# The adaLN modulation formed in two halves of the channels at the start of a hybrid conv and attention block

## The chip, the core and the metric

The kernel runs on one core of a Trainium2 chip. TensorE (PE) multiplies, VectorE (DVE), ScalarE (ACT) and GpSimd (POOL) do the rest, and SyncE (SP) and ACT issue most DMAs. The metric is the device time of one execution in microseconds; three runs gave 2390.78, 2391.32 and 2394.15, median 2391.32.

## The reference

One decoder block over 2048 tokens of 1024 channels in float32. What matters here is its beginning:

```python
mod = jax.nn.silu(c) @ w_ada + b_ada
shift, scale, gate = jnp.split(mod, 3, axis=-1)
h = (rms_norm(x, norm_w) * (1.0 + scale[:, None]) + shift[:, None]).astype(dt)
z = h @ w_in                     # (2048, 1024) @ (1024, 10240)
q = rope(rms_norm(q, q_norm_w), positions); k = rope(rms_norm(k, k_norm_w), positions)
```

`c` is one row of 1024, `w_ada` is 1024 x 3072; shift and scale, 2048 columns, are needed before any `h`. From `z` come a convolution branch, 12 attention heads of 128 channels in three groups of dilated windows, and the gates; two projections, the gated sum, `w_out` and the residual end the block.

## The kernel before

The contraction over 1024 channels is cut into KC = 8 slices of 128. A product in float32 is made of three with rounded parts: `h` and the weights are split into an upper part (`hi`, `wh`) and the remainder (`lo`, `wl`), and hi.wh + hi.wl + lo.wh are summed, 24 matmuls (name `pz`, line 373) for 128 tokens and the q, k and v of one head, 384 columns.

The order of PE is written out by hand (a manual schedule); the other engines are filled by a scheduler from the program order and from marks such as `keep_in_program_order`. A *unit* is one head, a *step* j is 128 tokens of it: unit 0 has 16 steps, and each step's `pz` is followed by squares on ACT (390), the power -1/2 on POOL (`rsqrt_cols`, 114 and 115), q and k norm and the rotation on DVE (404 to 414) and a store `qkv_d`. Tokens come in pairs of tiles: `load_x` loads x, squares it (261) and scales it by its norm (269) on ACT; `h_turn` transposes 256 tokens of two slices on PE (279) into a bank; `h_part` (and `h_first` for the first 256 tokens) modulates it out of the bank into `hf` on DVE (302; 290), rounds it to `hT_hi` on ACT (305; 285), subtracts for `hT_lo` (306; 292, half of these on POOL) and stores `hf` to `h_d` from SP. `hf` has two buffers. In unit 0 the parts for tokens j + 2 are made between the matmuls of step j.

The start: SP loads c, b_ada and norm_w as rows (`nat`), 16 blocks of w_ada (128 x 1024 each; two per slice), the positions and the frequencies; ACT's queue loads x0 to x3 and three blocks of w_in (`raw`). silu(c) is a column `sc` per slice. Of the eight slices of w_ada five are multiplied on PE, 1 x 512 into each of four banks (`ada`, 201); three are summed on DVE (192, 194) and then multiplied by a column of ones. Four copies on ACT (221) bring the row into SBUF, sixteen transposes (224) turn it into columns and two DVE operations give `mod` (225, 226). DVE also makes the angles of the rotary tables (`tab`, 165 to 175), ACT their sines (212, 213). Then the whole of `h` for the first 256 tokens is formed, in four calls of `h_first`, and step 0 begins. At its end unit 0 loads and splits the weights of unit 1 (343, 349, 352) through three `raw` buffers.

Of the kernel before, what the change touches and what calls it, by code (L numbers as in the profile page):

```python
# [10 lines left out]
F32 = mybir.dt.float32  # L11
# [43 lines left out]
def tile_hybrid_block(  # L55
# [67 lines left out]
    with pool("start", side="right") as st:  # L123
        keep = tc.keep_in_program_order
        nat = st.tile([4 * KC, P], F32, name="nat")
        cols = st.tile([P, 4 * KC], F32, name="cols")
        keep(nc.sync.dma_start(nat[:KC, :], c.rearrange("b (k p) -> (b k) p", p=P)))
        keep(nc.sync.dma_start(nat[KC : 3 * KC, :], b_ada[: 2 * D].rearrange("(k p) -> k p", p=P)))
        keep(nc.sync.dma_start(nat[3 * KC :, :], norm_w.rearrange("(k p) -> k p", p=P)))
        pos_i = st.tile([P, NB], I32, name="pos_i")  # L130
        freq = st.tile([P, 64], F32, name="freq")
        was = {}

        def ada_load(k):
            for half in range(2):
                wa = was[k, half] = st.tile([P, D], F32, tag="wa", name=f"wada{k}_{half}", bufs=10)
                last = keep(nc.sync.dma_start(wa, w_ada[P * k : P * k + P, D * half : D * half + D]))
            return last

        ada_load(0)  # L140
        keep(nc.sync.dma_start(pos_i, positions.rearrange("b (j p) -> p (b j)", p=P)))
        keep(nc.sync.dma_start(freq, inv_freq[None, :].to_broadcast([P, 64])))
        for k in range(1, KC):
            last_ada = ada_load(k)

        pt = bank("t", "pt_c")
        nc.tensor.transpose(pt[:, : 4 * KC], nat, ident[: 4 * KC, : 4 * KC])
        keep(nc.vector.tensor_copy(cols, pt[:, : 4 * KC]))
        th = consts.tile([P, KC], F32, name="th_c")
        with tc.high_priority():  # L150
            nc.scalar.activation(th, cols[:, :KC], AF.Tanh, scale=0.5)
        keep(nc.vector.scalar_tensor_tensor(sc, th, 1.0, cols[:, :KC], op0=ALU.add, op1=ALU.mult))
        keep(nc.vector.tensor_scalar(sc, sc, 0.5, None, op0=ALU.mult))

        pos_f = st.tile([P, NB], F32, name="pos_f")
        keep(nc.vector.tensor_copy(pos_f, pos_i))
        a = tab[:, :, 0, :]
        n = tab[:, :, 1, :]
        na = st.tile([P, NB, 64], F32, name="na")

        def angles():

            v = nc.vector

            yield v.tensor_tensor(a, pos_f[:, :, None].to_broadcast([P, NB, 64]),
                                  freq[:, None, :].to_broadcast([P, NB, 64]), op=ALU.mult)
            yield v.tensor_scalar(n, a, 1.0 / (2 * math.pi), MAGIC, op0=ALU.mult, op1=ALU.add)
            yield v.tensor_scalar(n, n, -MAGIC, None, op0=ALU.add)
            yield v.tensor_scalar(na, n, MAGIC * 2048, None, op0=ALU.add)
            yield v.tensor_scalar(na, na, -MAGIC * 2048, None, op0=ALU.add)  # L170
            yield v.tensor_sub(n, n, na)
            for part in TWO_PI:
                for t in (na, n):
                    yield v.scalar_tensor_tensor(a, t, -part, a, op0=ALU.mult, op1=ALU.add)
            yield v.tensor_scalar(a, a, -PI_LO, PI_LO, op0=ALU.max, op1=ALU.min)

        turning = angles()

        def angle_steps(count):
            for _, ins in zip(range(count), turning):  # L180
                keep(ins)


        BY_SUM = (1, 3, 5)
        acc = [bank("z", "ada0"), bank("z", "ada1"), bank("s", "ada2"), bank("s", "ada3")]
        sums = st.tile([P, 2 * D], F32, name="sums")

        def ada_sum(k):
            for half in range(2):
                part, wa = sums[:, D * half : D * half + D], was.pop((k, half))  # L190
                if k == BY_SUM[0]:
                    keep(nc.vector.tensor_scalar(part, wa, sc[:, k : k + 1], None, op0=ALU.mult))
                else:
                    keep(nc.vector.scalar_tensor_tensor(part, wa, sc[:, k : k + 1], part, op0=ALU.mult, op1=ALU.add))

        def ada_row(k):
            for half in range(2):
                wa = sums[:, D * half : D * half + D] if k is None else was.pop((k, half))
                col = ones[:, :1] if k is None else sc[:, k : k + 1]
                for i in range(2):  # L200
                    last_row = nc.tensor.matmul(acc[2 * half + i][:1, :], col, wa[:, 512 * i : 512 * i + 512],
                                                start=(k == 0), stop=(k == KC - 1))
# [12 lines left out]
        keep(nc.vector.tensor_scalar(a, a, -2.0, 1.0, op0=ALU.mult, op1=ALU.add))
        last_mm = {k: ada_row(k) for k in (0, 2, 4, None, 6, 7)}
        row = st.tile([1, 2 * D], F32, name="row")

        for i in range(4):
            with tc.issue_after(sin.ins):  # L220
                last_row = nc.scalar.activation(row[:, 512 * i : 512 * i + 512], acc[i][:1, :], AF.Copy)
        pa = bank("z", "pt_ada")
        for k in range(2 * KC):
            nc.tensor.transpose(pa[:, k : k + 1], row[:, P * k : P * k + P], ident[:1, :1])
        keep(nc.vector.tensor_add(mod, pa[:, : 2 * KC], cols[:, KC : 3 * KC]))
        keep(nc.vector.scalar_tensor_tensor(mod[:, KC:], mod[:, KC:], 1.0, cols[:, 3 * KC :], op0=ALU.add, op1=ALU.mult))
    hpool_c = [tc.tile_pool(name=f"hT{i}", bufs=1, side="right", reuse_waits="tile") for i in range(2)]
    hpools = [c.__enter__() for c in hpool_c]

    def quarter_tile(kh, t, hl, name, dtype=F32R):  # L230

        return hpools[0 if t == 0 or (kh, t) == (0, 2) else 1].tile([P, 4, 512], dtype, tag=f"h{hl}{kh}{t}", name=name)

    hi, lo = ({(kh, t): quarter_tile(kh, t, hl, f"hT_{hl}_{kh}{t}") for kh in range(2) for t in range(4)} for hl in ("hi", "lo"))

    def part(x, k, t0, w, nk=1):

        q = x[k // 4, t0 // 512]
        ks = k % 4 if nk == 1 else slice(k % 4, k % 4 + nk)
        return q[:, ks, t0 % 512 : t0 % 512 + w]  # L240
# [8 lines left out]
    def load_x(j, eng=nc.sync):  # L249
# [3 lines left out]
        if j >= 4:  # L253
            tc.keep_in_program_order(i0)
# [1323 lines left out]
```

## Time and profile before

| | us |
|---|---|
| median of three runs | 2391.32 |
| the profiled execution's own time | 2388.53 |
| its span in the profile | 2386.7 |
| PE busy, whole span | 2343.6 |
| first `pz` starts | 45.76 |
| step 4 of unit 0 starts | 73.90 |
| unit 1 starts | 139.55 |
| unit 1's step 1 starts | 147.73 |

All times in rows count from the span's start. A row of a timeline has the start, the duration, the engine, the line of the kernel, the operation, what it writes and reads with its shape, and in square brackets how long the engine was idle before it and what it waited for. Consecutive matmuls overlap, so the distance of their starts is the pace, not the duration. A row of the waits has the total, the number and the longest.

### The profile page before, as it was taken

The page shows a single profiled execution, that of the slowest core. Times are in us where ns is not written, and L with a number is a line of the kernel's source. Part 1 is how long each engine was busy: PE and PEld are TensorE (multiplying, and loading weights), DVE is VectorE, ACT ScalarE, POOL GpSimd, SP SyncE. Part 2 cuts the span into 40 slices and gives each one's busy share as a digit, 9 for nine tenths or more (in the row PEclk, how much of TensorE's full clock was granted, in tenths as well). Part 3 has the DMA queues.
Part 4 walks back from the last instruction along what each step waited for, and adds up shares of the span by engine and source line. Part 5 has one row for each costly group of instructions (what it writes and reads, how often), then busy time and mean ns, then how long its engine had stood idle before and what let it go on. Part 6 is the DMA issues. An engine that isn't in the chain of part 4 may idle for free.

```text
span 2386.7 us, 38725 instructions
## 1 busy us (share of the span) xinstructions
PE 2343.6 (98%) x12353; PEld 2088.3 (87%) x12353; DVE 1737.6 (73%) x4091; ACT 1024.4 (43%) x2850; POOL 843.8 (35%) x1003
## 2 busy tenths in 40 slices
PE   6999999999999999999999999999999999999999
PEld 2989999999999999998888888788888888878887
DVE  5865655555555777777699999979977778887654
ACT  4833433333444554456444444644444444333221
POOL 4421111111111111112577778755556730000221
PEclk9999999999999999999999999999999999999999
DMA  7633544544552222225545445744443569876552
GB/s 260 219 119 109 162 123 143 156 149 155 161 164 81 66 80 59 60 84 163 174 141 165 162 159 194 232 129 152 150 150 124 173 193 333 287 256 205 186 168 102
DMA packets 354106, 378.56 MB, mean 159 GB/s; under 512 B 29737, under 2 KB 251209, under 8 KB 353903
## 3 DMA queue, kind: packets, MB, share of 16 engines
q1 hardware_dynamic: 316414, 316.64, 42.1%
q10 hardware_dynamic: 37488, 59.46, 7.2%
q8 instruction: 98, 1.61, 0.3%
q14 instruction: 106, 0.86, 0.1%
HBM read 235.34 MB, written 140.64 MB: 158 GB/s over the span
## 4 chain that ended last, share of the span: by engine, by line
PE 89%; DVE 3%; DMA 3%; ACT 2%; POOL 1%; issue 1%; SPq 0%; ACTq 0%; DVEq 0%; POOLq 0%
PE pz L373 31%; PE paab L899 7%; PE yc L1207 5%; PE pcab L899 4%; PE pag_mc_d L899 4%; PE oa L1489 4%; PE pag_g_d L899 3%; PE ya L1207 3%; PE pag_ma_d L899 3%; PE po L502 3%; PE ps L453 3%; PE pcg_g_d L899 2%; PE oc L1489 2%; PE pbab L899 2%; PE paag L899 2%; PE pcg_mc_d L899 2%
## 5 line engine op out<-in xcount | busy, mean ns | idle before, releaser
L373 PE MATMUL pz<-wh_u,hT_lo 128*128 128x384 f32 x1536 | 537.6, 350 | 5.3 <-DVE hT_lo L292 3.8
L373 PE MATMUL pz<-wh_u,hT_hi 128*128 128x384 f32 x1536 | 518.9, 338 | 4.2 <-ACT wh_u L349 2.2
L373 PE MATMUL pz<-wl_u,hT_hi 128*128 128x384 f32 x1536 | 519.8, 338 | 0.6 <-DVE wl_u L352 0.4
L114 POOL TENSOR_SCALAR st<-st 128x2 f32<-128x2 f32 x192 | 48.3, 251 | 810.5 <-ACT sq L390 810.5
L404 DVE SCALAR_TENSOR_TENSOR qk<-pz,st,wqk 128x128 f32<-128x128 f32 x384 | 116.9, 346 | 272.3 <-POOL st L115 271.3
L373 PEld LDWEIGHTS pz<-wh_u,hT_lo 128*128 128x128 f32 x1536 | 289.6, 189 | 8.1 <-DVE hT_lo L292 4.6
L373 PEld LDWEIGHTS pz<-wh_u,hT_hi 128*128 128x128 f32 x1536 | 290.6, 189 | 6.6 <-ACT wh_u L349 2.8
L373 PEld LDWEIGHTS pz<-wl_u,hT_hi 128*128 128x128 f32 x1536 | 289.7, 189 | 1.8 <-DVE wl_u L352 1.3
L445 ACT ACTIVATE qkT<-ptq 128x256 f32<-128x256 f32 x192 | 73.9, 385 | 358.3 <-PE ptq L438 305.0
L977 DVE SCALAR_TENSOR_TENSOR ce<-us,pair_taps,ce 128x512 f32<-128x512 f32 x240 | 180.6, 753 | 6.4
L948 DVE SCALAR_TENSOR_TENSOR ce<-ut,chan,ce 128x512 f32<-128x512 f32 x240 | 178.9, 745 | 0.0
L863 POOL TENSOR_TENSOR slT<-wT,shT 128x512 fp32r<-128x512 f32 x107 | 143.9, 1346 | 79.9 <-ACT shT L862 76.7
L961 DVE SCALAR_TENSOR_TENSOR cq<-ut,chan,cq 128x512 f32<-128x512 f32 x208 | 155.3, 747 | 1.0
L862 ACT ACTIVATE shB<-wB 128x512 fp32r<-128x512 f32 x130 | 82.0, 631 | 161.3 <-PE paab L899 51.7
L390 ACT ACTIVATE sq<-pz 128x128 bf16<-128x128 f32 x384 | 105.9, 276 | 90.1 <-PE pz L373 80.8
L115 POOL TENSOR_TENSOR st<-st,mhalf 128x2 f32<-128x2 f32 x192 | 137.6, 717 | 16.0
L862 ACT ACTIVATE shT<-wT 128x512 fp32r<-128x512 f32 x110 | 69.4, 631 | 162.9 <-POOL wT L854 29.0
L863 POOL TENSOR_TENSOR slB<-wB,shB 128x512 fp32r<-128x512 f32 x85 | 111.2, 1309 | 76.9 <-ACT shB L862 76.2
L502 PE MATMUL po<-lv,pT 128*128 128x128 f32 x596 | 96.6, 273 | 0.0
L502 PEld LDWEIGHTS po<-lv,pT 128*128 128x128 f32 x596 | 91.0, 189 | 0.6 <-issue 0.5
L411 DVE TENSOR_TENSOR t<-qk,tab 128x256 f32<-128x256 f32 x192 | 82.4, 429 | 5.5
L863 POOL TENSOR_TENSOR slT<-wB,shT 128x512 fp32r<-128x512 f32 x57 | 74.9, 1321 | 27.7 <-ACT shT L862 27.7
(742 smaller groups left out, 6145.2 us busy)
## 6 DMA issues: line engine op xcount, KB each, us to landing
wB<-in_w_in_dram SPq DMA_DIRECT2D x154, 256.0 KB, 3.4
qkv_d<-qkv SPq DMA_DIRECT2D x128, 192.0 KB, 2.2
wT<-tT_d SPq DMA_DIRECT2D x88, 256.0 KB, 2.6
raw_u<-in_w_in_dram SPq DMA_DIRECT2D x93, 192.0 KB, 3.1
tT_d<-wB ACTq DMA_DIRECT2D x66, 256.0 KB, 2.2
lqk<-qkv_d SPq DMA_DIRECT2D x128, 128.0 KB, 2.2
acc_d<-osb SPq DMA_DIRECT2D x128, 65.0 KB, 1.9
part<-acc_d ACTq DMA_DIRECT2D x64, 130.0 KB, 2.2
```

The lines of the kernel that those rows point to most:

```text
L115: nc.gpsimd.tensor_tensor(dst, scratch[:, :n], mhalf[:, :n], op=ALU.pow)
L373: nc.tensor.matmul(pz[:, :width], part(a, k, P * j, P), w[:, :width], start=(m == 0), stop=(m == 23))
L404: nc.vector.scalar_tensor_tensor(qk[:, 2 * i : 2 * i + 2].rearrange("p a b -> p (a b)"), pz[:, P * i : P * i + P], st[:, 2 + i : 3 + i], w ...
L502: nc.tensor.matmul(po[:, :P], box["pT"][:, P * i : P * i + P], vt, start=(i == 0), stop=(i == nk - 1))
L862: nc.scalar.activation(h, q[name], AF.Copy)
L863: eng.tensor_tensor(l, q[name], h.bitcast(F32), op=ALU.subtract)
L899: nc.tensor.matmul(ps, w, x, start=(m == 0 and ps.name not in first), stop=(m == 11 and not more), skip_group_check=True)
L948: stt(box["e"], e[:, 1 + j : 513 + j], chan[:, cb, 2 * j : 2 * j + 1], box["e"], op0=ALU.mult, op1=ALU.add)
L961: stt(box["o"], o[:, 2 + j : 514 + j], w, psum_o, op0=ALU.mult, op1=ALU.add)
L977: stt(dst, box["both"][:, 1 + j : 513 + j], pair_taps[:, cb, j : j + 1], box["e"], op0=ALU.mult, op1=ALU.subtract if j == 0 else ALU.add)
L1207: nc.tensor.matmul(pz, w, xx, start=(m == 0), stop=(m == len(terms) - 1))
L1489: nc.tensor.matmul(ps, y, w, start=(m == 0 and ps.name not in begun), stop=(m == 11 and not more), skip_group_check=True)
```

## The change

The column vectors of shift and scale are formed by halves of the channels: half g holds channels 512g to 512g + 511 of both. A block of w_ada is now one slice's 512 shift and 512 scale columns of one half (512 KB, two runs of 2 KB a row). The stationary operand is `sc` copied to 32 columns (`wide`), and the 1024 results of a half go as four pieces of 256 columns to partitions 0, 32, 64 and 96 of one bank; one copy on ACT, two transposes on PE and the two DVE operations give that half of `mod`. Nothing is summed on DVE any more. All eight slices of the first half are loaded first; the blocks of w_in for unit 0, x2 to x5 and the second half's slices follow on SP's queue, and x0 and x1 stand at its head.

Between the halves PE transposes and multiplies what the first half's four slices of `h` allow for 512 tokens: steps 0 to 3 have a bank each (`first_pz`), and their matmuls go over two slices and two steps at a time. The rest follows behind the second half. The first half of tokens 4 and 5 is formed there as well. The positions are loaded as 16 rows and turned together with `nat`; the angles are made in two halves of 8 tiles, the second finished inside unit 0's steps. x0 to x5 are scaled half on ACT and half on DVE. The floats of the first 256 tokens have ten tiles of their own (borrowed from the pool `wk`), those of tokens 2 to 5 lie where w_ada landed. Unit 0 uses four banks for `pz`. From token 6 on the store of `hf` is issued by ACT. Of unit 1's blocks of w_in the first three are issued at the start, as before, and four more have tiles of their own.

```diff
+    def ada_load(g, k):
+        keep(nc.sync.dma_start(landed_ada(g, k), w_ada[P * k : P * k + P, : 2 * D].rearrange("p (s c) -> p s c", s=2)
+                               [:, :, 512 * g : 512 * g + 512]))
...
+    first_x(0)
+    first_x(1)
+    for k in range(2):
+        raw_load(k)
+    for k in range(KC):
+        ada_load(0, k)
+    for k in range(2, 4):
+        raw_load(k)
+    first_x(2)
+    first_x(3)
...
+    for k in range(4, KC):
+        raw_load(k)
+    for k in range(5):
+        ada_load(1, k)
+    first_x(4)
+    first_x(5)
+    for k in range(5, KC):
+        ada_load(1, k)
...
+    keep(nc.vector.tensor_copy(wide, sc[:, :, None].to_broadcast([P, KC, 32])))
...
+    def ada_mm(g, acc, k):
+        for q in range(4):
+            nc.tensor.matmul(acc[32 * q : 32 * q + 32, :256], wide[:, k], landed_ada(g, k)[:, q // 2, 256 * (q % 2) : 256 * (q % 2) + 256],
+                             start=(k == 0), stop=(k == KC - 1))
+
+    def ada_mod(g, acc, tag):
+        keep(nc.scalar.activation(rows[g], acc[:, :256], AF.Copy))
+        pa = bank(tag, f"pt_ada{g}")
+        for i in range(2):
+            nc.tensor.transpose(pa[:, P * i : P * i + P], rows[g][:, P * i : P * i + P], ident)
...
-                hf = xp.tile([P, 2, 256], F32, tag="hf", name=f"hf0_{k}", bufs=2)
+            order((nc.sync if order is keep else nc.scalar).dma_start(h_d[2 * kk : 2 * kk + 2, :, P * j : P * j + 256].rearrange("a p t -> p a t"), hf))
...
+    def first_z(j0, kk):
+        for m in range(3):
+            x, w = ((hi, "h"), (hi, "l"), (lo, "h"))[m]
+            for j in (j0, j0 + 1):
+                for k in (2 * kk, 2 * kk + 1):
+                    nc.tensor.matmul(first_pz[j][:, :384], part(x, k, P * j, P), split_w[w, k],
+                                     start=(k == 0 and m == 0), stop=(k == KC - 1 and m == 2))
...
+    ada_mod(0, acc, "o")
+    h_first(0)
+    first_w(2)
+    first_w(3)
+    h_first(1)
+    pair_square(2)
+    pair_square(3)
+    first_pz = [bank("z", f"pz0_{j}") for j in range(2)]
+    for kk in range(2):
+        first_z(0, kk)
+    angle_steps(1, 2)
+    for k in range(4, 6):
+        first_w(k)
+    pair_mean(2)
+    pair_scale(2)
+    pair_scale(3)
...
+    ada_mm(1, acc, 0)
+    h_parts(2, [(kk, h_turn(2, kk)) for kk in range(2)], keep)
+    for k in range(1, 4):
+        ada_mm(1, acc, k)
...
+    for kk in range(2):
+        first_z(2, kk)
...
+    ada_mm(1, acc, 4)
+    h_parts(4, [(kk, h_turn(4, kk)) for kk in range(2)], keep)
+    for k in range(5, KC):
+        ada_mm(1, acc, k)
...
+    ada_mod(1, acc, "o")
+    h_first(2)
+    h_first(3)
+    first_z(0, 2)
...
+            pz = bank("zzss"[j % 4] if u == 0 else "z", f"pz{n}")
...
-                    parts = (0, 1) if j % 2 == 0 else (2, 3)
+                    parts = () if j < 4 else (0, 1) if j % 2 == 0 else (2, 3)
...
+                    more_raw = open_side("rx")
+                if u == 0 and j == NB - 3:
+                    nxt, loads = unit_weights(1)
+                    for m, k in ((6, 0), (12, 1), (18, 2)):
+                        extra.setdefault(m, []).append(lambda k=k: early[-1](k))
```

In all three pairs below a name's last number is only its buffer's. PE from the first to the second half of the modulation: before, one modulation (`pt_ada`), then step 0.

```order
L201 MATMUL ada_174<-wada_1_159,sc 1x512
L224 MATMUL pt_ada<-ident,row 128x1 x16
L373 MATMUL pz_0_450<-wh_u_0_349,hT_hi_256 128x384
L373 MATMUL pz_0_450<-wl_u_0_350,hT_hi_256 128x384
L373 MATMUL pz_0_450<-wh_u_1_355,hT_hi_256 128x384
```

Now, with the rows between left out, `ada_260` being the first half's bank and `ada_392` the second's:

```order
L318 MATMUL ada_260<-first_lo_143,first_hi_134 32x256 x4
L325 MATMUL pt_ada_304<-ident,first_hi_134 128x128 x2
L381 MATMUL pz_0_341<-wh_u_0_241,hT_hi_199 128x384
...
L381 MATMUL pz_1_342<-wh_u_3_321,hT_lo_200 128x384
L318 MATMUL ada_392<-first_hi_136,first_hi_134 32x256 x4
L292 MATMUL pt_x_0_397<-ident,x_167 128x128
...
L381 MATMUL pz_3_444<-wh_u_3_321,hT_lo_200 128x384
L318 MATMUL ada_392<-first_lo_140,first_hi_134 32x256 x4
...
L325 MATMUL pt_ada_530<-ident,first_hi_134 128x128 x2
L381 MATMUL pz_0_341<-wh_u_4_369,hT_hi_201 128x384
```

Half of the matmuls of steps 0 to 3 have moved ahead of the second `pt_ada`, among the second half's slices. From step 4's first matmul on, all 11,145 rows of PE are the same in both.

ACT around step 2's squares, where x7 is scaled (`x_524`; `x_442` is x5 before). Before:

```order
L390 ACTIVATE sq_0_504,st_0_505<-pz_0_450 128x128 x2
L400 ACTIVATE qkv_0_508<-pz_0_450 128x128
L261 ACTIVATE xn_444,xst_445<-x_442 128x512
L305 ACTIVATE hT_hi_256<-hf_0_473 128x2x256
L269 ACTIVATE x_438<-x_438,xst_441 128x512
```

Now:

```order
L577 ACTIVATE sq_2_724,st_2_725<-pz_2_443 128x128
L266 ACTIVATE xn_716,xst_575<-x_573 128x512
L367 ACTIVATE hT_hi_613<-first_lo_140 128x2x256
L274 ACTIVATE x_524<-x_524,xst_526 128x512 x2
L577 ACTIVATE sq_2_724,st_2_725<-pz_2_443 128x128
L274 ACTIVATE x_573<-x_573,xst_575 128x512 x2
L587 ACTIVATE qkv_2_728<-pz_2_443 128x128
L266 ACTIVATE xn_741,xst_578<-x_576 128x512
L577 ACTIVATE sq_3_749,st_3_750<-pz_3_444 128x128
L367 ACTIVATE hT_hi_473<-hf_0_783 128x2x256
L371 DMA h_d<-hf_0_783 128x2x256
```

The scale of x7 stands behind step 2's first square and the last `hT_hi` of tokens 4 (`hT_hi_613`), and each `hT_hi` from token 6 on is followed by the store of its `hf`.

SP before unit 1's weights, at the end of unit 0. Before, blocks 3 to 5 behind the store of step 13 and 6 and 7 behind that of step 14:

```order
L789 DMA qkv_d<-qkv_13_1453 128x384
L343 DMA raw_u_3_1504<-in_w_in_dram 128x3x128
L343 DMA raw_u_4_1542<-in_w_in_dram 128x3x128
L343 DMA raw_u_5_1554<-in_w_in_dram 128x3x128
L610 DMA ch_nat<-in_conv_ln_b_dram 1x1024
L789 DMA qkv_d<-qkv_14_1523 128x384
L343 DMA raw_u_6_1563<-in_w_in_dram 128x3x128
```

Now behind those of steps 12 and 13:

```order
L973 DMA qkv_d<-qkv_12_1392 128x384
L520 DMA raw_more_1483<-in_w_in_dram 128x3x128
L520 DMA raw_more_1485<-in_w_in_dram 128x3x128
L520 DMA raw_more_1487<-in_w_in_dram 128x3x128
L973 DMA qkv_d<-qkv_13_1462 128x384
L520 DMA raw_more_1489<-in_w_in_dram 128x3x128
L520 DMA raw_u_7_1518<-in_w_in_dram 128x3x128
```

Blocks 3 to 7 stand one store earlier. On DVE, POOL, ACT and SP too the rows are the same from unit 1's step 1 on.

431 lines of the change are left out of this document (261 added, 170 removed).

## The prediction

> **What bounds the kernel now.** I read the busy time by stage first, cut at events of the program, then PE's timeline and the waits of the stages in which PE isn't full.
>
> ```profile
> 0.00:45.70 45.70, 28.57 (x81) 7.22 (x81) 26.40 (x29) 21.50 (x43) 20.30 (x31) 0.96 0.84 295
> 45.70:58.59 12.89, 8.85 (x32) 6.81 (x33) 5.35 (x12) 6.75 (x15) 4.08 (x7) 0.80 0.46 157
> 58.59:73.90 15.31, 15.31 (x83) 15.07 (x83) 12.74 (x31) 12.54 (x38) 6.00 (x12) 0.83 0.44 148
> 73.90:139.55 65.65, 63.38 (x385) 60.44 (x383) 57.27 (x147) 44.92 (x137) 27.66 (x51) 1.00 0.63 211
> 139.55:147.73 8.18, 5.42 (x26) 3.99 (x25) 4.49 (x12) 3.19 (x10) 1.03 (x2) 1.00 0.36 111
> 147.73:2387.00 2239.27, 2222.07 (x11753) 1994.72 (x11752) 1631.38 (x3862) 935.48 (x2611) 784.67 (x900) 1.00 0.49 155
> ```
>
> After the stretch come its length, the busy time of PE, PEld, DVE, ACT and POOL, the clock, the DMA share and GB/s. The last stretch is 99% PE, and in the changed kernel all five engines issue that part in the same order. So the change is worth what it moves one event: the start of unit 1's step 1, at 147.73 us. Before it lie the fill (no pz before 45.7), steps 0 to 3 of unit 0 (to 73.90), steps 4 to 15 (to 139.55) and unit 1's step 0. The timeline of PE and the waits of the first 60 us show the fill:
>
> ```profile
> 35.85 5.31 PE L201 MATMUL ada<-wada,sc 128*1 128x512 f32 x12
> 45.76 0.44 PE L373 MATMUL pz<-wh_u,hT_hi 128*128 128x384 f32 x1 [1.27 <-ACT hT_hi L285]
> 47.16 0.52 PE L373 MATMUL pz<-wl_u,hT_hi 128*128 128x384 f32 x1
> 47.48 0.52 PE L373 MATMUL pz<-wh_u,hT_hi 128*128 128x384 f32 x1
> ...
> 50.33 0.34 PE L373 MATMUL pz<-wl_u,hT_hi 128*128 128x384 f32 x1
> 50.50 0.33 PE L373 MATMUL pz<-wh_u,hT_hi 128*128 128x384 f32 x1
> ```
> ```profile
> DVE hf L290 <- DMA h_d<-hf: 5.9, 3, 3.5
> PE pz L373 <- DVE hT_lo L292: 3.8, 3, 1.5
> ```
>
> The whole modulation has to be there before the first pz. Then PE catches up, and is held again: h_first's hf has two buffers, DVE waits for their stores (5.9 us), PE for DVE. Starts of pz are 0.32 us apart after a pause and 0.17 in steady running (24 of them in 4.15 us at the full clock). A step with its 8 transposes is (73.90 - 58.59)/3 = 5.10.
>
> ```profile
> 139.55 0.33 PE L373 MATMUL pz<-wh_u,hT_hi 128*128 128x384 f32 x1
> ...
> 142.18 0.45 PE L373 MATMUL pz<-wh_u,hT_hi 128*128 128x384 f32 x1 [0.90 <-ACT wh_u L349]
> ```
>
> Unit 1's step 0 takes 8.18 us, 4.03 over 4.15: its weights come late. Steps 4 to 15 take 65.65, where ten steps of 5.10 and two of 4.15 are 59.3: 6.35 is stall.
>
> **The change part by part.** *Loads.* The price of a packet comes from the table of queues: 0.421 x 16 x 2386.7 us over 316,414 packets is 50.8 ns for 1,001 bytes, and 73.3 ns for 1,586 on the other.
>
> ```profile
> q1 hardware_dynamic: 316414, 316.64, 42.1%
> q10 hardware_dynamic: 37488, 59.46, 7.2%
> ```
> ```profile
> 10.00:15.00 5.00, 3.99 (x7) 0.55 (x5) 0.00 (x0) 3.31 (x8) 1.96 (x4) 1.00 0.98 307
> 15.00:20.00 5.00, 0.54 (x1) 0.09 (x2) 4.43 (x7) 3.55 (x9) 3.55 (x4) 0.93 1.02 415
> ```
> ```profile
> 4.51 0.63 ACT L261 ACTIVATE xn<-x 128x512 bf16<-128x512 f32 x1 [0.53 <-DMA x<-in_x_dram]
> ```
>
> The line through both gives an estimated 256 GB/s for raw (512-byte runs) and 360 for the halves of w_ada (2 KB runs); rows of 4 KB are seen at 415. Here x0 is issued at 0.72 and lands at 4.51; in the change it stands behind four small loads of 0.4 us, so I put it at 6.1. Then x1, two raws and eight first halves: 1.3 + 1.5 + 11.6 us, landed at 20.5. Behind them two raws 1.5 (22.0), x2 and x3 2.6 (24.6), norm weights 0.5, four raws 3.1 (28.2), five second halves 7.3 (35.5), x4 and x5 2.5 (38.0), three halves 4.4: 42.4. The positions' 2,048 runs of 4 bytes, which lie in the 307 GB/s stretch, become 16 rows. Lower bound 415 GB/s for the halves (2.6 us less by the end), upper bound 307 for all 13.2 MB: some 6 more.
>
> *First modulation.* The last slice's four pieces of 256 columns are 4 x 0.215 (half of 5.31/12), 21.4; then one copy, two transposes and two DVE operations, 1.4 by these rows, 22.8. Before, the same way takes 4.0 (41.16 to 45.11): four copies with weight splits between them.
>
> ```profile
> 43.46 0.57 ACT L221 ACTIVATE row<-ada 1x512 f32<-1x512 f32 x1
> 44.53 0.17 DVE L225 TENSOR_TENSOR mod<-pt_ada,cols 128x16 f32<-128x16 f32 x1 [1.24 <-PE pt_ada L224]
> 44.74 0.37 DVE L226 SCALAR_TENSOR_TENSOR mod<-mod,cols 128x8 f32<-128x8 f32 x1
> 45.15 3.76 ACT L285 ACTIVATE hT_hi<-pt_x,mod 128x256 fp32r<-128x256 f32 x8 [1.11 <-DVE mod L226]
> ```
>
> *Between the halves.* PE's 24 first pz (4.2 to 7.7 us) end by 31 and are not on the path; x2 and x3 are. ACT: six operations of 0.45 (25.5), four squares of 0.6 (27.9), two splits (28.8). POOL has two weight splits ahead of the power: 1.0 each alone, 1.83 beside a busy DVE; I take 1.0, since DVE is mostly idle there (30.3), the power 0.7 (31.0).
>
> ```profile
> 10.07 0.99 POOL L352 TENSOR_TENSOR wl_u<-raw_u,wh_u 128x384 fp32r<-128x384 f32 x1
> 34.63 3.66 POOL L352 TENSOR_TENSOR wl_u<-raw_u,wh_u 128x384 fp32r<-128x384 f32 x2 [9.60 <-ACT wh_u L349]
> 25.07 1.34 ACT L269 ACTIVATE x<-x,xst 128x512 f32<-128x512 f32 x2 [4.02 <-POOL xst L115]
> ```
> ```profile
> L115 POOL TENSOR_TENSOR st<-st,mhalf 128x2 f32<-128x2 f32 x192 | 137.6, 717 | 16.0
> ```
>
> Scales 1.3, eight transposes 0.9 (33.2), three slices of w_ada at 0.86 (35.8), 24 pz (40.0). x4 and x5, landed at 38.0, are squared by 39.2, scaled by 41.5, turned by 42.4, just as the last slice lands. The three slices left take PE to 45.0; copy, transposes and DVE's queue (four modulations, two subtractions and two angle steps from 42.0 on: 4.5 us) put the second mod at 47.1, two us after the only one of before. But 48 of the 96 pz of steps 0 to 3, with half their transposes, are done by then.
>
> *Second half.* 48 pz 8.3, 16 transposes 1.8, the first hT_hi 0.5, waits for hT_lo 1.0, and 1.5 for pz at the slow pace (ten of them): 60.2. The ten tiles for the floats take the wait for stores away. Before, PE is here at 73.90: 13.7 us of lead.
>
> On the column pieces the Trainium skill (TensorE: Matmul & The Clock Gate, Packing small matmuls) says that pieces at different column strips run at once, measured 2.38 times for three; by that, an estimate, the six slices on this way would be some 2 us shorter, and the time 2372. Against it stands the Trainium skill's TensorEngine Tiling (Key Properties): a change of the tiling drains the array, here at each group of slices. No run here shows either.
>
> *Steps 4 to 15.* The pz of steps 0 to 3 come to ACT and DVE in a bunch. One step of DVE in steady running:
>
> ```profile
> 26.97 1.23 DVE L174 SCALAR_TENSOR_TENSOR tab<-na,tab 128x1024 f32<-128x1024 f32 x1
> ...
> 90.48 0.61 DVE L404 SCALAR_TENSOR_TENSOR qk<-pz,st,wqk 128x128 f32<-128x128 f32 x2
> 91.00 0.98 DVE L302 TENSOR_SCALAR hf<-pt_x,mod 128x256 f32<-128x256 f32 x2
> 91.91 0.41 DVE L411 TENSOR_TENSOR t<-qk,tab 128x256 f32<-128x256 f32 x1
> 92.24 0.42 DVE L412 TENSOR_TENSOR qkv<-qk,tab 128x256 f32<-128x256 f32 x1
> 92.58 0.68 DVE L306 TENSOR_TENSOR hT_lo<-hf,hT_hi 128x512 fp32r<-128x512 f32 x1
> 93.18 0.28 DVE L413 TENSOR_TENSOR qkv<-qkv,t 128x128 f32<-128x128 f32 x1
> ```
>
> From start to start, a part of h is 0.91 + 0.60 and a step's qkv 0.52 + 0.33 + 0.34 + two of 0.2, so 1.6; two parts and a qkv are 4.6 of the 5.10, room 0.5. First the chain into step 4: the last part of tokens 4 is turned at 60.2, DVE modulates it behind step 0's qkv (1.6 + 0.9: 62.7), ACT makes hT_hi (0.5) and then scales x7 (1.3): 64.5. PE wants x7 for its transposes eleven pz after 60.2, at 62.1: I take 2.5 us of wait, bounds 0 (if ACT comes to x7 first) and 5 (twice). Then the backlog: four qkv of 1.6 and five angle operations on half the width (1.23/2 each at most, 3.1) are 9.5 us, ten steps have room for 4.9, and 4.6 is left. Four banks for pz instead of two carry some of it, and stalls of the old kind (6.35 before) may stay: I take 4.0, bounds 0 and 9.5. ACT issues the stores of h now, 20 in ten steps; such an issue hides under the operation that runs (ACT's next one starts 0.52 us after the last, with the issue between):
>
> ```profile
> 1506.16 0.62 ACT L727 ACTIVATE A_hi<-landingA 128x512 fp32r<-128x512 f32 x1
> 1506.29 0.33 ACTq L1026 DMA_DIRECT2D ma_d<-spare_hi  x1
> 1506.68 0.62 ACT L862 ACTIVATE shT<-wB 128x512 fp32r<-128x512 f32 x1
> ```
>
> Nothing, then; without that cover 20 x 0.33 = 6.6 us of ACT.
>
> *Unit 1's weights.* Three raws are issued in the fill, as before; four now have places of their own and stand one store earlier on SP: 4.15 for step 0, bounds 4.15 and 8.18.
>
> *Sum.* 60.2 + 2.5 + 59.3 + 4.0 + 4.15 = 130.2 against 147.73: 17.5 us. The profiled execution took 2388.53, its span 2386.7; the median shown lies 2.8 above it. 2391.3 - 17.5 = 2373.8, so **2374 us**.
>
> **The rivals.** *The fill is later.* With 307 GB/s and POOL's splits at 1.83, the second mod comes 6 to 8 us later: 2381. For it: 307 is seen with mixed loads; against: the 4-byte runs that were among them are gone. *DVE sets unit 0.* All 9.5 us of backlog come out as stall: 5.5 more, 2379; with the stall of unit 1 kept (4.0), 2383. For it: no room is left beside 4.6 of 5.10 if anything is late; against: two more banks. *No pause.* No slow pace (1.5), no wait in step 4 (2.5), no stall behind it (4.0): 8 us less, 2366. For it: PE never rests over 2 us from 33 us on. *The change doesn't do what it says:* the first half's work can't start before x2 and x3 and the second mod waits for all of it, so what is left is the stores' wait and the weights, 5.9 + 4.0, less 2 for the later mod: 8 us, 2383. For it: x2 lands only at 24.6; against: ACT and POOL have little else then. *Slower:* the ring of hf. In the change its store stands on ACT behind hT_hi, and DVE waits for it two parts later.
>
> ```profile
> h_d<-hf SPq DMA_DIRECT2D x28, 256.0 KB, 2.1
> ```
>
> A round of two buffers (a step) is 0.9 for the modulation, the time w until ACT comes to it, 0.3 to issue, 2.1 to land: 3.4 + w. It sets the step from w = 1.7, and outweighs 17.5 us over ten steps from a step of 6.85, w = 3.5. ACT's 44.92 busy us of 65.65 in these steps speak against so long a queue, the bunch of four steps for it; at w = 4.2 a step is 7.6, 25 us more: 2399.
>
> **How the numbers follow.** Forecast 0.56 (2368 to 2378), later fill 0.12, DVE 0.12, no pause 0.08, not what it says 0.05, slower 0.05; 0.02 for no change by a mixture of them. Range 2365 to 2385. About 0.2% (4.8 us) is what can be told from no change: faster 0.89, same 0.06 (that 0.02, and 0.04 of the cases at 2383, should they run a little further), slower 0.05.
>
> **What would show it.** First pz near 23 us, second mod near 47, steps 0 to 3 and tokens 4's transposes done near 60; a PE wait on x's scale in step 4; unit 0 over near 126, no wait on wh_u in unit 1. The forecast is wrong if the second mod comes after 55, if steps 4 to 13 take more than 6 us each, or if the stretch behind unit 1's step 1 is not 2239 us.

## The result, and the profile after

The changed kernel takes 2378.98 us (median of four runs, 2378.02 to 2379.51) against 2391.80 for the kernel before (four runs, 2390.78 to 2394.15): a ratio of 0.9945, 95% interval 0.9927 to 0.9962. That is 12.8 us less. The two profiled executions differ by 9.0 us (2388.53 and 2379.51): the start is 11.9 us shorter, and the last stretch, behind unit 1's step 1, 2.9 us longer. The prediction said 2374 with a range of 2365 to 2385: the sign and the range held, and some 5 us of the expected gain are missing.

The busy time by stage of the changed kernel, cut at its own events: first `pz`, first `pz` behind the second modulation, step 4, unit 1, unit 1's step 1. The columns are those of the first fence of the prediction.

```profile
0.00:22.81 22.81, 8.08 (x75) 2.66 (x76) 16.50 (x36) 10.06 (x21) 5.00 (x15) 1.00 0.89 326
22.81:46.86 24.05, 18.75 (x139) 14.34 (x139) 19.20 (x36) 14.85 (x35) 9.68 (x10) 0.93 0.99 353
46.86:59.31 12.45, 12.00 (x64) 11.58 (x65) 7.34 (x16) 7.47 (x23) 4.26 (x10) 0.86 0.68 230
59.31:131.68 72.37, 63.47 (x371) 59.61 (x370) 60.98 (x160) 49.83 (x152) 31.02 (x53) 0.98 0.56 183
131.68:135.84 4.16, 4.16 (x25) 4.16 (x25) 3.22 (x9) 1.51 (x7) 1.14 (x2) 1.00 0.43 133
135.84:2377.70 2241.86, 2223.92 (x11753) 1995.76 (x11752) 1633.18 (x3866) 935.79 (x2611) 785.74 (x900) 1.00 0.49 154
```

Unit 1's step 1 starts at 135.84 instead of 147.73, a lead of 11.9 us; 17.5 were forecast (130.2). Everything up to step 4 came as expected or a little sooner (59.31 against a forecast of 60.2), and unit 1's step 0 takes 4.16. The loss is in one row, the fourth: steps 4 to 15 take 72.37 us, where the matmuls and transposes alone need 59.3. That is 13.1 us of stall; the forecast had 6.5 (2.5 for x7 and 4.0 for the rest).

The kernel before lost 4.1 us there, not 6.35. Its step 4 starts at 76.19 and not at 73.90, the figure of the table and the prediction: the prediction's row from 73.90 to 139.55 has 385 operations on PE, the row from 76.19 has 370, and these steps have 371 in the changed kernel.

```profile
76.19:139.55 63.36, 61.09 (x370) 58.19 (x369) 54.98 (x141) 43.54 (x134) 26.68 (x48) 1.00 0.62 207
```

So the change is 16.9 us ahead when step 4 starts, and steps 4 to 15 give 9.0 of them back.

The waits of PE in that stage, then those of ACT and of DVE (total, number, longest):

```profile
PE pt_x L292 <- ACT x L274: 4.6, 3, 2.7
PE pz L554 <- DVE hT_lo L369: 2.6, 3, 1.3
PE pz L554 <- ACT hT_hi L367: 1.3, 2, 1.1
PE pt_x L292 <- issue: 0.4, 1, 0.4
...
ACT x L274 <- POOL xst L115: 8.7, 5, 2.3
...
DVE qk L591 <- POOL st L115: 4.3, 4, 2.0
DVE hf L364 <- DMA h_d<-hf: 0.9, 2, 0.6
```

PE's waits add up to 8.9 us; the rest of the 13.1 is the slow pace that can follow a wait (in step 8, after 89.69, starts of `pz` are 0.32 us apart instead of 0.17). Counted from the first `pz` of one step to that of the next, steps 4 to 15 take 6.83, 5.09, 8.46, 5.11, 9.32, 5.10, 6.76, 5.10, 7.09, 5.11, 4.24 and 4.16 us. Only even steps lose, those that need a new pair of x. And behind ACT's scale of x (line 274) stands POOL: 8.7 us of waits for three operations on 128x1 numbers.

What POOL was doing there is seen when its rows are laid beside DVE's. First just before step 6, which starts at 71.23:

```profile
67.29 2.85 POOL L269 TENSOR_TENSOR xst<-xst 128x1 f32<-128x1 f32 x1 [2.18 <-ACT xn L266]
70.23 0.23 POOL L114 TENSOR_SCALAR xst<-xst 128x1 f32<-128x1 f32 x1
...
66.48 0.99 DVE L364 TENSOR_SCALAR hf<-pt_x,mod 128x256 f32<-128x256 f32 x2
67.39 0.42 DVE L221 TENSOR_SCALAR tab<-tab 128x512 f32<-128x512 f32 x1
67.72 0.42 DVE L598 TENSOR_TENSOR t<-qk,tab 128x256 f32<-128x256 f32 x1
68.06 0.42 DVE L599 TENSOR_TENSOR qkv<-qk,tab 128x256 f32<-128x256 f32 x1
68.39 0.69 DVE L369 TENSOR_TENSOR hT_lo<-hf,hT_hi 128x512 fp32r<-128x512 f32 x1
68.99 0.28 DVE L600 TENSOR_TENSOR qkv<-qkv,t 128x128 f32<-128x128 f32 x1
69.20 0.28 DVE L601 TENSOR_TENSOR qkv<-qkv,t 128x128 f32<-128x128 f32 x1
69.40 0.69 DVE L369 TENSOR_TENSOR hT_lo<-hf,hT_hi 128x512 fp32r<-128x512 f32 x1
...
71.44 1.34 ACT L274 ACTIVATE x<-x,xst 128x512 f32<-128x512 f32 x2 [2.26 <-POOL xst L115]
```

The add of one number a partition, 0.2 us elsewhere, ends at 70.14, just as DVE's unbroken row of operations on SBUF ends (70.09). DVE itself then stands still for 2.0 us, waiting for POOL's norm of q and k (the longest wait in its row for line 591 above), and in step 6 PE waits twice for `hT_lo`. In step 8 it is the epsilon's turn, and here the chain to PE is complete:

```profile
86.13 2.10 POOL L114 TENSOR_SCALAR xst<-xst 128x1 f32<-128x1 f32 x1
...
88.92 1.33 ACT L274 ACTIVATE x<-x,xst 128x512 f32<-128x512 f32 x2 [2.12 <-POOL xst L115]
...
89.69 0.90 PE L292 MATMUL pt_x<-ident,x 128*128 128x128 f32 x3 [2.71 <-ACT x L274]
```

Just before step 12, which starts at 111.08, the POOL operation ends while DVE goes on without a pause:

```profile
110.23 1.73 POOL L269 TENSOR_TENSOR xst<-xst 128x1 f32<-128x1 f32 x1 [0.88 <-ACT xn L266]
...
109.95 0.68 DVE L369 TENSOR_TENSOR hT_lo<-hf,hT_hi 128x512 fp32r<-128x512 f32 x1
110.55 0.42 DVE L598 TENSOR_TENSOR t<-qk,tab 128x256 f32<-128x256 f32 x1
110.89 0.41 DVE L599 TENSOR_TENSOR qkv<-qk,tab 128x256 f32<-128x256 f32 x1
111.22 0.68 DVE L369 TENSOR_TENSOR hT_lo<-hf,hT_hi 128x512 fp32r<-128x512 f32 x1
111.83 0.99 DVE L364 TENSOR_SCALAR hf<-pt_x,mod 128x256 f32<-128x256 f32 x2
```

It ends at 111.96, when the last operation with two operands in SBUF is over (111.90) and DVE has turned to one that reads a PSUM bank. So what holds POOL seems to be not that DVE is busy but what it reads.

### The profile page after: what moved, and what is told of

The parts are those of the page before. It is cut to its first block, busy times and chain, and to the rows that moved or that the text cites. A ratio compares the mean times of both kernels' runs of the same rounds, so it can differ in the third digit from the quotient of the medians.

```text
span 2377.7 us, 38834 instructions
## 1 busy us (share of the span) xinstructions
PE 2330.4 (98%) x12421; PEld 2088.1 (88%) x12421; DVE 1740.4 (73%) x4118; ACT 1019.5 (43%) x2845; POOL 836.8 (35%) x989
## 4 chain that ended last, share of the span: by engine, by line
PE 84%; DVE 4%; DMA 4%; ACT 1%; issue 1%; POOL 1%; SPq 0%; ACTq 0%; POOLq 0%; DVEq 0%
PE pz L554 29%; PE paab L1083 7%; PE yc L1391 6%; PE pcab L1083 4%; PE pag_mc_d L1083 4%; PE oa L1673 4%; PE pag_g_d L1083 3%; PE pag_ma_d L1083 3%; PE po L689 3%; PE ps L640 2%; PE pcg_g_d L1083 2%; PE oc L1673 2%; PE pbab L1083 2%; PE paag L1083 2%; PE pcg_mc_d L1083 2%; PE ptq L625 2%
## 5 line engine op out<-in xcount | busy, mean ns | idle before, releaser
L554 PE MATMUL pz<-wh_u,hT_lo 128*128 128x384 f32 x1504 | 524.5, 349 | 2.6 <-DVE hT_lo L369 2.6
L554 PE MATMUL pz<-wh_u,hT_hi 128*128 128x384 f32 x1504 | 505.6, 336 | 1.3 <-ACT hT_hi L367 1.3
L554 PE MATMUL pz<-wl_u,hT_hi 128*128 128x384 f32 x1504 | 506.4, 337 | 0.0
L554 PEld LDWEIGHTS pz<-wh_u,hT_lo 128*128 128x128 f32 x1504 | 283.2, 188 | 4.1 <-DVE hT_lo L369 3.7
L554 PEld LDWEIGHTS pz<-wh_u,hT_hi 128*128 128x128 f32 x1504 | 283.7, 189 | 2.6 <-ACT hT_hi L367 2.2
L554 PEld LDWEIGHTS pz<-wl_u,hT_hi 128*128 128x128 f32 x1504 | 282.6, 188 | 0.5 <-issue 0.5
```

The lines of the kernel that those rows point to most:

```text
L554: nc.tensor.matmul(pz[:, :width], part(a, k, P * j, P), w[:, :width], start=(m == 0), stop=(m == 23))
```

## The experiments

Theory P: POOL's small operations for the norm of x are held by DVE's row; ACT, in order, stands behind them, and PE behind ACT. Theory D, the prediction's own rival: DVE has more work in these steps than fits. All kernels below are the changed kernel with one edit (the last one has four). They are compared by the profiled execution, by the event "unit 1's step 1 starts". An edit also lets the scheduler place the rows of DVE and ACT near it in another order, and the fill alone moves step 4 by about 1 us from one execution to the next (59.25 to 60.31 in the kernels below whose fill is unchanged).

The slow pace after a wait also comes in one execution and not in another. Step 8 has the same wait of 2.7 us in the changed kernel, weights_late, exp_later and one_strip, but it takes 9.3 to 9.4 us in the first two, with a granted clock of 0.82, and 8.0 to 8.1 in the other two, at 1.00. This 1.3 us belongs to no edit. The step in the changed kernel and in exp_later:

```profile
84.79:94.12 9.33, 6.62 (x33) 6.28 (x33) 5.94 (x18) 5.36 (x16) 4.84 (x8) 0.82 0.61 200
```
```profile
84.72:92.75 8.03, 5.32 (x33) 4.97 (x33) 5.89 (x18) 5.36 (x16) 4.60 (x8) 1.00 0.59 200
```

| kernel | time, us | step 4 at | steps 4 to 15 | unit 1's step 0 | event at |
|---|---|---|---|---|---|
| before | 2391.80 | 76.19 | 63.36 | 8.18 | 147.73 |
| changed | 2378.98 | 59.31 | 72.37 | 4.16 | 135.84 |
| no_pool_x | 2370.40 | 58.36 | 66.37 | 4.16 | 128.89 |
| no_angle | 2379.24 | 61.42 | 66.16 | 4.16 | 131.74 |
| exp_later | 2378.51 | 59.25 | 68.92 | 4.16 | 132.33 |
| stores_sp | 2383.00 | 59.73 | 74.50 | 5.35 | 139.58 |
| mean_dve | 2379.43 | 60.29 | 72.50 | 4.16 | 136.95 |
| angle_gap | 2380.64 | 58.56 | 71.31 | 4.16 | 134.03 |
| one_strip | 2390.24 | 71.69 | 71.36 | 4.16 | 147.21 |
| no_early_pz | 2382.79 | 66.71 | 70.56 | 4.16 | 141.43 |
| x_ahead | 2376.56 | 59.44 | 68.91 | 4.16 | 132.51 |
| weights_late | 2389.82 | 60.31 | 72.16 | 10.86 | 143.33 |
| two_banks | 2382.10 | 60.10 | 73.67 | 4.16 | 137.93 |
| combined | 2376.14 | 58.66 | 66.34 | 4.16 | 129.16 |

Times are medians for before, changed and combined, and single executions for the rest. A time is the event plus a last stretch that varies by 7 us (last section), so single times within some us of each other tell nothing; the events tell more, to within 1 or 2 us.

**No POOL in the way of x.**

```diff
-                nc.gpsimd.tensor_add(st[:, 0:1], st[:, 0:1], st[:, 1:2])
-                rsqrt_cols(st[:, 1:2], st[:, 0:1], 1, st[:, 2:3])
...
-            return nc.scalar.activation(xt[:, halves[i]], xt[:, halves[i]], AF.Copy, scale=st[:, 1:2])
+            return nc.scalar.activation(xt[:, halves[i]], xt[:, halves[i]], AF.Copy, scale=ones[:, 1:2])
```

> All expectations go by one event, the start of unit 1's step 1, at 135.8 us in the changed kernel (147.7 before). This kernel leaves out the mean and the power of x6 to x15: POOL's three small operations for each are gone, and ACT scales x by a column of ones. Theory P (POOL's small operations for the norm of x are held as long as DVE issues operations on two operands in SBUF without a pause; ACT's scale waits behind them in order, and PE behind ACT): the stalls of steps 6, 8 and 12 (3.4 + 4.2 + 2.0 us over 5.10) go for the most part, event at 127 to 130. Theory D (DVE simply has more work in steps 4 to 13 than fits, the backlog of the prediction): those stalls stay or move to waits on hf and hT_lo, event at 134 to 136.

The event comes at 128.89, 6.95 us earlier, in the range of P. DVE does nearly the same work in this stage, 59.89 us against 60.98:

```profile
58.36:124.73 66.37, 62.26 (x371) 60.03 (x370) 59.89 (x157) 49.79 (x152) 20.28 (x28) 0.97 0.61 199
```

The stalls of steps 8, 10 and 12 are gone (5.42, 5.10 and 5.51 us for the three), step 6 keeps 1.3 of 3.4, and step 4 loses 3.9, since there x7's scale stands behind `hT_hi` on ACT and not behind POOL. POOL's norm of x thus costs 5 to 6 of the 13.1 us (6.0 with the slow pace of step 8, 4.7 without), and 7.1 us of stall stay.

**No rest of the angles.** The last three steps of the second half, its end and its two sines are left out.

```diff
-    angle_steps(1, 20)
-    angle_sine(1)
...
-    at_step(0, 5, 14, lambda: angle_end(1))
```

> Leaves out what is left of the second half of the angles after the second modulation: three operations and the two of the end on DVE (2.9 us), two sines on ACT (1.3 us). Theory D: DVE's backlog shrinks by 2.9 us and the stall with it, start of unit 1's step 1 at 133 or earlier. Theory P: only the first of the three holds (67.29 us, 2.85 long) loses some of its cover, the ones before steps 8 and 12 stay: 134 to 136.

Steps 4 to 15 take 66.16, 6.2 us less, twice the DVE time removed; the event, at 131.74, would have been near 129.6 had step 4 not started 2.1 us later here. So D's lever works too. But look at what went with it, ACT's wait for POOL:

```profile
ACT x L274 <- POOL xst L115: 4.0, 3, 2.1
```

It is 4.0 us, where the changed kernel has 8.7. P and D are two links of one chain: a denser DVE leaves fewer gaps for POOL. Neither alone is the cause, and taking out either link gives about half. The edit also takes 1.3 us of sines off ACT, which this run can't tell apart from DVE's part, and no run takes out both links at once.

**The Exp table later.**

```diff
-    at_step(0, 9, 14, lambda: keep(nc.scalar.activation(th[:, :1], th[:, :1], AF.Exp)))
+    at_step(1, 2, 14, lambda: keep(nc.scalar.activation(th[:, :1], th[:, :1], AF.Exp)))
```

> The load of the Exp table (1.28 us on ACT at 101.0, in step 9) is moved to unit 1's step 2. Theory E (the load makes ACT late for step 10's hT_hi): the 1.7 us that step 10 loses go, start of unit 1's step 1 at 134.2. Theory P: the load only stood in a wait that comes anyway with the next norm of x on POOL: 135 to 136.

The event is 3.5 us earlier, more than E said, but not where E said: step 10 still takes 6.49 (6.76 before the edit), now waiting for `hT_lo`. What went is step 12's stall (5.09 instead of 7.09) and 1.3 us of slow pace in step 8, ahead of the table load, which is not the edit's (above). That leaves some 2 us for the edit, by the load or by the new order of rows behind it; its mechanism isn't settled.

**Stores back on SP.**

```diff
-            order((nc.sync if order is keep else nc.scalar).dma_start(h_d[...], hf))
+            order(nc.sync.dma_start(h_d[...], hf))
```

> All stores of hf go back to SP. Theory S (the 20 issues on ACT, 0.37 us each, and the ring of hf behind them cost time): ACT gains up to 7.4 us, start of unit 1's step 1 at 131 to 133. Theory P (the issues lie beside other work and the ring isn't what PE waits for): 135 to 136.5, or a little later where the store on SP now stands behind the store of a qkv.

Both theories missed: 3.7 us later, 1.2 of it in unit 1's step 0 (5.35). SP holds stores that wait, and behind them now stand qkv's store and the load of x. ACT then waits for a qkv buffer (a row of its waits), squares x later, and PE stands in step 8 (a row of its timeline), which takes 12.12 us:

```profile
ACT qkv L587 <- DMA qkv_d<-qkv: 3.4, 4, 1.6
...
91.87 0.90 PE L292 MATMUL pt_x<-ident,x 128*128 128x128 f32 x3 [4.61 <-ACT x L274]
```

The stores on ACT, the prediction's one way to a loss, are a gain.

**The mean on DVE.**

```diff
-                nc.gpsimd.tensor_add(st[:, 0:1], st[:, 0:1], st[:, 1:2])
-                rsqrt_cols(st[:, 1:2], st[:, 0:1], 1, st[:, 2:3])
+                nc.vector.tensor_scalar(st[:, 2:3], st[:, 0:1], st[:, 1:2], EPS, op0=ALU.add, op1=ALU.add)
+                nc.gpsimd.tensor_tensor(st[:, 1:2], st[:, 2:3], mhalf[:, :1], op=ALU.pow)
```

> For x6 to x15 the mean (sum of two halves plus epsilon) is one operation on DVE instead of two on POOL; the power stays on POOL. Theory P: the operations that were held (2.85, 1.05, 2.10 and 1.73 us) were the sum and the epsilon, so three of the stalls shrink: start of unit 1's step 1 at 130 to 133 (135.8 in the changed kernel). Rival P2: whichever operation POOL comes with next is held as long, now the power: 135 to 136.5.

No gain (136.95), a little worse than P2 said. The hold passes to POOL's next customer, the norm of q and k, and the mean now queues on the very engine that is behind; step 8 takes 12.68:

```profile
80.66 2.14 POOL L114 TENSOR_SCALAR st<-st 128x2 f32<-128x2 f32 x1 [5.76 <-ACT sq L577]
...
91.61 0.69 PE L292 MATMUL pt_x<-ident,x 128*128 128x128 f32 x2 [4.78 <-ACT x L274]
```

Not all of that wait is POOL's: the scale that PE waits for starts at 90.85 on ACT, behind a copy (line 587) that had waited 1.17 us for a `qkv` buffer. So this run alone does not decide between P and P2.

**Angles in DVE's gaps.** Behind the second modulation DVE idles 2.77 us before 51.98 and 1.77 before 57.04.

```diff
-    angle_steps(1, 2)
     ada_mod(1, acc, "o")
     h_first(2)
     h_first(3)
+    angle_steps(1, 3)
...
+    angle_steps(1, 20)
     first_z(2, 2)
...
-    angle_steps(1, 20)
     angle_sine(1)
```

> The two angle steps ahead of the second modulation and the three after it on DVE are moved into DVE's two gaps behind it (2.77 us before 51.98 and 1.77 us before 57.04). The second modulation should come 1.0 us earlier (DVE stood at angles until 45.8, its transposes were done at 44.6). Theory D+P (DVE's dense run behind step 4 is what holds POOL): also 1.8 us less in the dense run, start of unit 1's step 1 at 131 to 133. Rival: only the 1.0 us of the modulation comes through: 134.8.

The event is 1.8 us earlier, between the two; the second modulation comes 0.5 us earlier, not 1.0. Steps 6 and 8 lose almost nothing now (5.80 and 5.11), as D+P has it; but the work put into the gaps makes tokens 4 late, x7's scale stands behind them, and step 4 takes 11.52.

**All pieces on one strip.**

```diff
-            nc.tensor.matmul(acc[32 * q : 32 * q + 32, :256], wide[:, k], ...
-                             start=(k == 0), stop=(k == KC - 1))
+            nc.tensor.matmul(acc[:32, :256], wide[:, k], ...
+                             start=(k == 0 and q == 0), stop=(k == KC - 1 and q == 3))
```

> All four pieces of a slice go to the same 32 columns of the array and the same part of the bank, so that they can't run side by side; the values of the modulation are wrong by this (the four pieces are added up), the work is the same. Theory C (pieces at different column strips run at once): a slice, eight records, takes four times what it takes in the changed kernel, about 1.7 us against 0.45 at the full clock; between the first and second modulation five slices lie on the way, so the start of unit 1's step 1 is 5 to 8 us later: 141 to 144. Rival: the pieces ran one after another before too, a slice stays at 0.45: 135.8.

The copy to SBUF then takes only these 32 rows. Three slices, 24 records (a float32 matmul has two), in the changed kernel and then on one strip:

```profile
41.59 1.50 PE L318 MATMUL ada<-first_lo,first_hi 128*32 128x256 f32 x24
43.02 1.09 PE L301 MATMUL pt_first<-ident,x 128*128 128x128 f32 x8
```
```profile
40.52 5.37 PE L321 MATMUL ada<-first_hi,first_hi 128*32 128x256 f32 x24
```

(43.02 - 41.59)/3 = 0.48 us a slice against 5.37/3 = 1.79: four pieces at four column strips run 3.7 times as fast as one behind another. The event comes 11.4 us later, more than expected since the first half's last slices wait too (step 4 at 71.69); the stalls of steps 4 to 15 keep their pattern, but for the pace in step 8. The rule of the Trainium skill (TensorE: Matmul & The Clock Gate, Packing small matmuls) that such pieces run at once holds here, and with four pieces more comes out than its 2.38 for three; a drain between transposes and slices does not show in these rows.

**No early pz.** The 48 matmuls between the two modulations move behind the second one.

```diff
-    for kk in range(2):
-        first_z(0, kk)
...
-    for kk in range(2):
-        first_z(2, kk)
...
-    first_z(0, 2)
+    for kk in range(3):
+        first_z(0, kk)
...
-    first_z(2, 2)
+    for kk in range(3):
+        first_z(2, kk)
```

> The 48 matmuls of steps 0 to 3 that stood between the two modulations are moved behind the second; the transposes and the forming of h stay where they are. If PE's early work is what was won (the prediction), 48 x 0.173 = 8.3 us come back, and PE paces slowly before it, start of unit 1's step 1 at 144 to 146. Rival (unit 0 is set by DVE, POOL and ACT anyway, the early matmuls only wait later): the stalls of steps 4 to 15 (13.1 us) shrink by what PE comes later: 136 to 139.

In between: step 4 starts 7.4 us later, but steps 4 to 15 take 1.8 us less, and 5.6 us arrive at the event. Some of the early work is paid back as stall, and most of it is real.

**Norms of x ahead.** The squares of x come one to two steps sooner, the two scales a step behind the squares.

```diff
-                    for m, f in zip((4, 4, 9, 12), normed.pop(j + (6 if j < 4 else 4), ())):
+                    steps = normed.pop(j + (6 if j < 6 else 5), ())
+                    for m, f in [(4, f) for f in steps[:2]] + list(zip((2, 6), normed.pop("scale", ()))):
                         extra.setdefault(m, []).append(lambda f=f: tc.keep_in_program_order(f()))
+                    normed["scale"] = steps[2:]
```

> From step 4 on the squares of x come one to two steps sooner, and the two scales of an x one step behind its squares, so that POOL has a whole step for the norm and ACT doesn't stand at a scale. Theory P with slack (what costs is that a late POOL operation meets ACT's queue in order): the waits on x's scale in steps 8 and 12 and the one before step 10 go, 4 to 7 us, start of unit 1's step 1 at 129 to 132. Rival (the work of ACT and DVE as a whole doesn't fit; where x stands in it only moves the waits, as the mean on DVE did): 134.5 to 137.

The event is 3.3 us earlier (132.51), short of P's 4 to 7 and well off the rival. PE's waits now:

```profile
PE pz L554 <- DVE hT_lo L369: 4.8, 5, 1.3
PE pt_x L292 <- ACT x L274: 1.4, 1, 1.4
PE pz L554 <- ACT hT_hi L367: 0.8, 2, 0.5
```

The waits on x are gone but for step 4's; POOL is still held, up to 2.8 us, and it no longer matters for x. In its place DVE's own `hT_lo` comes late, 4.8 us in place of 2.6: with P's link mended, D's shows.

**Unit 1's weights late, and two banks.**

```diff
-                        for k in (3, 4, 5, 6):
-                            extra.setdefault(0, []).append(
-                                lambda k=k: early[-1](k, more_raw.tile([P, 384], F32, tag=f"more{k}", name=f"raw_more{k}", bufs=1)))
-                        extra.setdefault(16, []).append(lambda: early[-1](7))
```

> Unit 1's blocks 3 to 7 of w_in are loaded through the three old buffers again instead of four places of their own. By the prediction's term unit 1's step 0 takes about 8.2 us again instead of 4.16, the rest stays: start of unit 1's step 1 at 139.9. Rival (unit 0 now ends with ACT and DVE less loaded, so the three buffers come free in time): 136 to 137.5.

```diff
-            pz = bank("zzss"[j % 4] if u == 0 else "z", f"pz{n}")
+            pz = bank("z", f"pz{n}")
```

> From step 4 on unit 0 uses two banks for pz instead of four. If the two more banks carry DVE's backlog, PE now also waits for a bank: 3 or more us later, start of unit 1's step 1 at 139 or later. Rival (PE's waits in steps 4 to 13 are on x, hT_hi and hT_lo, none on a bank): 135.5 to 137.

Unit 1's step 0 takes 10.86 us with the late weights, 6.7 more than 4.16, where the prediction's term was 4.0: the event is 7.5 us later (143.33; 139.9 was expected). With two banks PE waits 6.07 us for a bank ahead of step 6, and then step 8 has no stall: 2.1 us in all (137.93, between the two expectations). A row of each:

```profile
137.74 0.50 PE L554 MATMUL pz<-wh_u,hT_hi 128*128 128x384 f32 x1 [3.54 <-ACT wh_u L531]
```
```profile
78.25 0.66 PE L554 MATMUL pz<-wh_u,hT_hi 128*128 128x384 f32 x1 [6.07 <-DVE qk L591]
```

**Combined:** the norms ahead, the Exp table later, the angles in the gaps, and

```diff
-    h_parts(4, [(3, h_turn(4, 3))], keep)
+    pts = [(3, h_turn(4, 3))]
     for f in ready[1][2:]:
         keep(f())
+    h_parts(4, pts, keep)
```

> Four edits together: the norms of x ahead (alone 3.3 us earlier at the start of unit 1's step 1), the Exp table in unit 1 (alone 3.5), the angles in DVE's gaps (alone 1.8), and x7's scale ahead of the last hT_hi of tokens 4 on ACT (the wait in step 4, 1.7 us). If they are waits of their own the sum is 10.3 us: event at 125.5, time 2368 to 2370. If, as the single runs suggest, they are links of one chain in which the next wait takes over part of what is won: 128 to 131, time 2371 to 2375. Rival: no better than the best alone, 132 to 133, 2376.

The event comes at 129.16, 6.7 us before the changed kernel's: the middle case, links of one chain. The time is 2376.14 (median of six, 2372.56 to 2378.70), not the 2371 to 2375 of that case: in the profiled execution the last stretch is 2246.1 us, the longest of all. The kernel before took 2393.49 beside it: 0.992, 95% interval 0.9905 to 0.9935. Against the changed kernel's 0.9945 the intervals overlap, so that it is faster than the changed kernel is likely but not shown.

## Why the prediction was right, and where not

**Fill and both modulations: right.** First `pz` 22.81 (forecast near 23), the second modulation at 46.14 (47.1), steps 0 to 3 done at 59.31 (60.2):

```profile
22.81 1.37 PE L381 MATMUL pz<-wh_u,hT_hi 128*128 128x384 f32 x4 [1.55 <-ACT hT_hi L339]
...
46.86 0.44 PE L381 MATMUL pz<-wh_u,hT_hi 128*128 128x384 f32 x1 [2.27 <-ACT hT_hi L339]
...
45.98 0.16 DVE L330 SCALAR_TENSOR_TENSOR mod<-mod,first_hi 128x4 f32<-128x4 f32 x1
```

Two prices under it were wrong. The estimate of 360 GB/s for runs of 2 KB was too low; between 10 and 20 us the core moved 402:

```profile
10.00:20.00 10.00, 7.02 (x72) 2.28 (x72) 8.76 (x16) 4.91 (x8) 3.34 (x3) 1.00 1.06 402
```

And a slice on PE was put at four times half a record, 0.86. The row it came from lists each float32 matmul twice, so that pieces one behind another would be 1.79; side by side they are 0.48. The sum was saved by luck, by an effect that it did not count on: with the pieces one behind another the event is 11 us later, as the one-strip kernel shows. Two side estimates, which are not in the sum, don't come out either: 16 halves at 415 instead of 360 GB/s are 3.1 us less, not 2.6, and six slices of 0.86 made 2.38 times faster are 3.0 us shorter, not some 2. The lead of 13.7 us was counted from 73.90; from 76.19 it is 16.0, and the old stall of 6.35 is 4.1. The forecast time does not change by these, since it is added up from the start of the changed kernel.

**The wait on x7 in step 4: right in mechanism**, 1.73 us lost in that step against 2.5.

```profile
63.01 0.55 PE L292 MATMUL pt_x<-ident,x 128*128 128x128 f32 x3 [1.41 <-ACT x L274]
```

**"Stall of steps 4 to 15, 4.0": the step that failed.** It was 11.3 behind step 4 (13.1 less 1.7), 7.3 more than put in and above the stated upper bound of 9.5. With it two of the prediction's own signs of being wrong came: steps 4 to 13 took 6.40 us each on average (its bound was 6), and the last stretch was not 2239 us. The backlog of DVE was seen; the working let it be carried by free room of 0.5 us a step and by two more banks, and treated POOL as an engine with time to spare (45% busy or less in every stage). What was missed: POOL's small operations are on the way of x, they are held up by DVE's operations that read only SBUF, and a backlog makes those come without a gap. Each hold of 1.7 to 2.9 us then goes through ACT's order, or through DVE's own wait for POOL, to PE, which can go on slowly after it. The rival "DVE sets unit 0" gave 2379, the measured time, but with a stall of 9.5 us, not 11.3; its mechanism is one link, since with DVE's work nearly unchanged and POOL out of the way 5 to 6 of the 13.1 us go.

**Unit 1's step 0 at 4.15: right** (4.16), and worth 6.7 us in this kernel. **The other rivals:** no later fill; the slow pace and pauses stayed, so not 2366; the early work came before the second modulation. The ring of `hf` cost DVE 0.9 us of waits in all, and ACT's stores proved better than SP's. **The last stretch** took 2241.86, not 2239.0 (the 2239.27 of the prediction's row runs 0.3 us past the end of the span); the order there is the same. PE is idle 1.0 us more in it, its waits for `red` being 2.7 us instead of 0.7 (last section), and busy 1.9 us more.

## What to carry to other kernels

An engine that is 40% busy can still set the pace, if its operations are short, on the way of something, and locked out by a neighbour: look at the longest row of an operation that is usually short, and lay the neighbour's rows beside it. Work that is made early has to be consumed at the same rate everywhere; what arrives in a bunch takes away the gaps in which other engines did their small work. And give such side chains a step of slack rather than moving them to the engine that is already late.

## What the runs showed of the hardware that was not expected

POOL often waits out a whole run of DVE operations, not one. The Trainium skill (SBUF — State Buffer, Who interferes with whom) says that a DVE operation with two SBUF inputs shares a port with GpSimd, and that whoever starts first holds it for the whole instruction. The traces agree on the kind of operation (the hold ends at 111.96 when DVE turns to a bank), but in the long holds the loser does not get in between two instructions: 2.85 us at 67.29 spans seven that read only SBUF, six of them with two operands there. The kernel before has the same, a 2.38 us operation at 125.11. It is not so every time. In the kernel before an epsilon ends at 118.68, when one `hT_lo` (117.92 to 118.60) is over, though the next two operations on SBUF follow without a gap:

```profile
118.04 0.64 POOL L114 TENSOR_SCALAR xst<-xst 128x1 f32<-128x1 f32 x1
...
118.52 0.42 DVE L411 TENSOR_TENSOR t<-qk,tab 128x256 f32<-128x256 f32 x1
118.86 0.42 DVE L412 TENSOR_TENSOR qkv<-qk,tab 128x256 f32<-128x256 f32 x1
```

Up to unit 1, every sum or epsilon held for more than 1.3 us, in all fourteen profiles, ends with the run. What decides between the two is open.

The last stretch, with the same order of instructions in every kernel but for the table load, took from 2239.0 to 2246.1 us over the fourteen profiled executions. One wait late in it varies along; in the kernel before and in the combined one:

```profile
PE pc L1243 <- DVE red L1237: 0.7, 1, 0.7
```
```profile
PE pc L1430 <- DVE red L1424: 3.8, 1, 3.8
```

So part of what is won at the start may be lost again 1900 us later. Whether an earlier start makes that wait longer or it varies by itself, one profiled execution of each kernel can't tell: the earliest event with the short wait (128.89, 1.4 us) and with the long one (129.16, 3.8 us) lie side by side.
